# Six key projections of a hybrid decoder block: computed ahead by seven products and read back

## The chip, the core and the metric

The kernel runs on one core of a Trainium2 chip. The metric is the time of one execution on the device in microseconds (us); the lower the better. Five engines work side by side, each through its own instructions in order: TensorE (PE; its weight loads are shown as PEld), VectorE (DVE), ScalarE (ACT), GpSimd (POOL) and SyncE (SP), whose queue issues most DMAs here. They hand work over with semaphores.

## The reference, cut to what matters

A decoder block over 1024 tokens of 1024 channels: a normalised input h, a wide projection of h into many parts, two token mixers (retention over chunks, and dilated window attention in three groups of four heads), gates, and an MLP. The change concerns the keys of the attention, `ak`, 128 columns of the projection for each head:

```python
proj = h @ w_in                       # (1024, 1024) @ (1024, columns)
aq, ak, av = parts[4 + 3 * gi], parts[5 + 3 * gi], parts[6 + 3 * gi]      # per group gi
s = einsum(qs, kb) * (dh ** -0.5) + bias          # scores in a window, per head
p = exp(s - max(s)) / sum;  o = einsum(p, vb)     # groups merged by log-sum weights afterwards
```

## The kernel before, in words

Every float32 matrix product is made of three products of rounded halves (`mm3`, L215): each operand is split into a high half (a rounding copy on ScalarE) and a low half (a subtraction on VectorE), and TensorE adds low x high, high x low and high x high in PSUM. `split_w` (L206) does this for a weight tile of 128 x 1024.

Two ways of projecting stand in the kernel. The **direct** one (`proj_mm`, L503; `proj_gen`, L508) projects h on 128 columns: 8 k-steps of 6 matmuls, 48 matmuls of 512 columns. The other one, in the **queries' stage** (`queries_keys`, L1186, with the class `Blocks`, L238), takes two such column blocks at once as a 2 x 2 block product with seven products instead of eight: 7 x 4 x 3 = 84 matmuls for what costs 2 x 48 = 96 directly. Its operands from h are sums made once (`XA`); those from the weights are summed and split on VectorE and ScalarE while TensorE works (`prep`, L249), and results are combined on the way out of PSUM (`post`, `a_out`, L1136) and written to DRAM. `PAIRS` (L1110) lists what it computes: retention queries and keys ("r"), half of the retention gates ("s"), the attention's queries ("a"), and branch gates ("g"); 22 pairs.

The stages run in this order: attention values of group 0 and of groups 1 and 2, queries' stage, retention values, retention over 4 heads x 8 chunks (`chunk`, L748), attention, attention output, retention output, output projection, MLP.

The **attention** runs twice, for a pair of heads each (`pair` 0 and 1). In a pair there are six combinations of group g and head a (`combos`, L1767): (1,0) (1,1) (2,0) (2,1) (0,0) (0,1). `att_step(pair, i)` (L1769) projects the keys of combination i directly and, woven between the k-steps (`weave`, L524), computes the scores of combination i-1 (`scores_gen`, L1481): three PSUM banks of scores for group 1, two for group 2, four for group 0, each bank followed by the addition of the bias on VectorE (L1508, L1512). Behind that stand `k_split` (L1473), which splits the new keys out of PSUM, and `scores_end` (L1515): maxima on VectorE (L1518 to L1526), their negation `ng` (L1528), and eight exponentials on ScalarE (L1531). `cover_step` (L1809) does the same beside a gate's direct projection; its steps 0 and 1 cover the last scores, the weights of the groups (`weights`, L1601) and the scaling of P (`pscale`, L1632), and from step 2 on the products with the values (PV; `pv_stream`, L1701) are woven with gate projections. Pair 0's PV ends in the first step of pair 1.

What a step needs from DRAM stands in its list of loads. `Steps.run` (L71) keeps three raw tiles of 512 KB in flight on SP: a new load is issued when an earlier tile has been split (`prepare`, L93). For a step that isn't `manual`, `prepare` splits the loads of the next step, and the weights of the one after, ahead of the body. For a `manual` step the body gets a function, `args[0]`, and what it is given is split where the body calls it: `args[0](3)` splits the loads of the next step at that place. Instructions are issued in the order in which the program writes them, on every engine. Before, all steps of `att_step` but the first of each pair, and `cover_step` 0, are not manual.

The bias tables (`bias_load`, L1442) are six small DMAs issued at the end of each pair's first step. The `result_sums` (L612) prepare operands of the retention output: for the last half of the channels eight DMAs from DRAM to DRAM on POOL, four copies and four accumulations, which were issued in a row in the first attention step (L1789).

Of the kernel before, what the change touches and what calls it, by code (L numbers as in the profile page):

```python
# [21 lines left out]
H = 4  # L22
# [111 lines left out]
def block_kernel(ctx, tc, io, stop=None, dbg=None):  # L134
# [716 lines left out]
    aq_d = {(p, g, a): dram.tile([P, S], F32, name=f"aqd{p}{g}{a}") for p in range(2) for g in range(3) for a in range(2)}  # L851
    h12_d = [dram.tile([P, 2, 512], F32, name=f"h12d{m}") for m in range(4)]
# [257 lines left out]
    PAIRS = [{"r": r_pairs, "a": a_pairs, "g": g_pairs, "s": s_pairs}[i].pop(0) for i in "rsrarsrarsrarsraggagga"]  # L1110
# [3 lines left out]
    def a_load(q, part):  # L1114
        pair = PAIRS[q]
        src = io[{"g": "w_gate2", "a": "w_aq", "s": "w_rg2"}.get(pair[0]) or f"w_r{pair[1]}"]
# [19 lines left out]
    def a_out(q, n, x, y=None):  # L1136
# [6 lines left out]
        if pair[0] == "a" and pair[1] == 1:  # L1143
            o = OA[q][i].rearrange("p (r n i) -> p r n i", r=4, n=2)[:, :, t, :]
            view = lambda z: z.rearrange("p (i r) -> p r i", r=4)
        elif pair[0] == "a" and pair[1] == 2:
            o = OA[q][i].rearrange("p (r i) -> p r i", r=8)[:, :, 64 * t:64 * t + 64]
            view = lambda z: z.rearrange("p (i r) -> p r i", r=8)
# [223 lines left out]
    r_loads = {(0, 0): [io["w_rg"][0]], (H - 1, 7): [io["w_ak"][4]]}  # L1372
# [91 lines left out]
    def q_prep(pair, g, a):  # L1464

        def prep(raw):
            hi, lo = ring(f"qh{pair}{g}{a}"), ring(f"ql{pair}{g}{a}")
            nc.scalar.mul(hi, raw, QSCALE)
            nc.vector.scalar_tensor_tensor(lo, raw, QSCALE, fv(hi), op0=ALU.mult, op1=ALU.subtract)
            A["q", g, a] = (hi, lo)  # L1470
        return prep
# [297 lines left out]
    def att_step(pair, i):  # L1769

        g, a = combos[i]

        def body(*args):
            ps = ps_mm(f"ak{pair}{i}")
            gen = proj_gen(ps, hd.pop("w") if i == pair == 0 else args[-1])
            if i == len(combos) - 2:
                v_fetch(pair, 0)
            if i > 0:
                last = combos[i - 1]
                weave(gen, NK, scores_gen(pair, *last), len(SB[last[0]]), lag=2)  # L1780
            elif pair == 0:
# [13 lines left out]
            if i == 0:  # L1795
                A["st"] = A["p"].tile([P, 3, 8, 4], F32, tag="st", name=f"st{pair}")
                bias_load(pair)
            later_loads()
            if i == 0 and pair == 1:
                banks_sc()  # L1800
            else:
                k_split(pair, g, a, ps)
            if i > 0:
                scores_end(pair, *last)
                if last[1] == 1:
                    stats_out(pair, last[0])
        return body

    def cover_step(pair, n):  # L1809


        i = COVER[pair][n]

        def body(*args):
            if n == 2:
                banks_pv((("mm", "ac2", "ac3", "s", "ac0", "ac1"), ("ac0", "ac1", "s", "ac2", "ac3", "mm"))[pair])
                v_fetch(pair, 2)
            ps = ps_mm(f"gate0{i}")
            gen = proj_gen(ps, args[-1])
            if n == 0:  # L1820
                v_fetch(pair, 1)
                weave(gen, 6, scores_gen(pair, *combos[-1]), len(SB[0]), lag=2, rest=False)
                drain(gen)
                later_loads()
                for j in range(2):
                    vs_high(pair, 0, j)
                t = ring(f"g0{i}s", F32)
                nc.scalar.copy(t, flat(ps))
                A["gate", 0] = t, t
                scores_end(pair, *combos[-1])  # L1830
                weights(pair)
                pscale(0, 0)
            elif n == 1:
                drain(gen)
# [9 lines left out]

    for pair in range(2):
        for i, (g, a) in enumerate(combos):
            steps.add(att_step(pair, i),
                      ([] if i == pair == 0 else [wsplit(io["w_ak"][g * 4 + 2 * pair + a])]) +
                      ([(aq_d[pair, *combos[i - 1]], q_prep(pair, *combos[i - 1]))] if i > 0 else []),
                      manual=i == 0)  # L1850
        for n in range(len(COVER[pair])):
            more = [(aq_d[pair, *combos[-1]], q_prep(pair, *combos[-1]))] if n == 0 else []
            steps.add(cover_step(pair, n), more + [wsplit(io["w_gate"][len(COVER[0]) * pair + n])], manual=n > 0)
# [860 lines left out]
def pack(x, c, w_ada, b_ada, norm1_g, w_in, rel_bias, ret_gn_g, ret_gn_b,  # L2714
# [3 lines left out]
    att = w[:, 6144:10752].reshape(1024, 3, 3, 512)  # L2718
    rg = w[:, 4096:6144].reshape(1024, 4, 512)
# [16 lines left out]
        "w_ak": _cols(att[:, :, 1].reshape(1024, 1536)),  # L2736
# [29 lines left out]
```

## Time and profile before

| | |
|---|---|
| median of 3 runs | 2183.61 us (2181.96 to 2184.4) |
| the profiled execution's own time | 2182.82 us |
| its span in the trace | 2181.1 us |
| granted TensorE clock, mean | 0.998 |
| queries' stage | about 149 to 568 us of the span |
| attention | about 942 to 1251 us |

A row of the timeline has the start, the time from the first start to the last end of the merged instructions, engine, line, operation, output<-inputs, shape and count, and in brackets the idle time before it and what ended it. A row of a group (by tile) has minimum/median/maximum in ns and the first and last start. A row of windows has the busy time of each engine in the stretch with the number of instructions, then the granted clock, the DMA engines' busy share and GB/s. TensorE's pipelined matmuls overlap in such rows, so the distance of starts is the price of one, not its duration.

### The profile page before, as it was taken

What the parts mean: (1) busy time and instruction counts of PE and PEld (TensorE: products, weight loads), DVE (VectorE), ACT (ScalarE), POOL (GpSimd) and SP (SyncE); (2) the same over time, 40 slices, a digit from 0 to 9 for tenths busy, and PEclk for the clock granted to TensorE, in tenths of its full rate; (3) what the DMA queues carried; (4) which work ended last, traced back from release to release, by engine and by line L of the source; (5) the groups of instructions that cost most, each with busy time, mean ns of one, the idle gap of its engine ahead of it and who ended that gap; (6) DMA issues with size and microseconds to landing.
All of it is one profiled execution on the core that took longest, in us unless ns stands there. A gap on an engine that the chain in (4) does not pass through costs nothing.

```text
span 2181.1 us, 27045 instructions
## 1 busy us (share of the span) xinstructions
PE 2147.4 (98%) x10034; PEld 1784.6 (82%) x10034; DVE 1479.0 (68%) x2281; ACT 947.1 (43%) x1715; POOL 178.4 (8%) x192
## 2 busy tenths in 40 slices
PE   7999999999999999999999999999999999999998
PEld 5888888888888888888888888888878888788887
DVE  6756777767566678854655644677876665887855
ACT  4533322333334566654644525434554455433412
POOL 0101111100000334410000000001000000000003
PEclk9999999999999999999999999999999999999999
DMA  9869998734687758977323366653054445645322
GB/s 382 231 193 297 289 328 266 217 136 155 223 297 287 257 181 242 263 222 186 105 81 108 98 250 210 224 184 130 35 202 159 154 143 188 240 138 173 109 87 78
DMA packets 161891, 422.55 MB, mean 194 GB/s; under 512 B 27734, under 2 KB 55645, under 8 KB 157662
## 3 DMA queue, kind: packets, MB, share of 16 engines
q1 hardware_dynamic: 151902, 372.57, 48.4%
q0 software_dynamic: 9856, 48.24, 10.1%
q8 instruction: 79, 1.29, 0.2%
q14 instruction: 54, 0.44, 0.1%
HBM read 325.71 MB, written 160.32 MB: 223 GB/s over the span
## 4 chain that ended last, share of the span: by engine, by line
PE 90%; DVE 4%; ACT 2%; DMA 1%; issue 1%; POOL 0%; SPq 0%; POOLq 0%; DVEq 0%; ACTq 0%
PE qap L219 6%; PE qap L223 6%; PE qap L221 6%; PE fp L219 4%; PE fp L223 4%; PE fp L221 4%; PE ak L219 2%; PE ak L221 2%; PE ak L223 2%; PE f2a L221 2%; PE f2a L223 2%; PE f2a L219 2%; PE rg L221 1%; PE rg L219 1%; PE rg L223 1%; PE va L221 1%
## 5 line engine op out<-in xcount | busy, mean ns | idle before, releaser
L219 PE MATMUL qap<-hh,qaw 128*128 128x512 f32 x264 | 102.8, 389 | 0.1
L221 PE MATMUL qap<-hl,qaw 128*128 128x512 f32 x264 | 102.7, 389 | 0.0
L223 PE MATMUL qap<-hh,qaw 128*128 128x512 f32 x264 | 102.7, 389 | 0.0
L656 POOL TENSOR_TENSOR j<-qk,j 128x512 fp32r<-128x512 f32 x32 | 48.3, 1513 | 311.7 <-ACT j L655 311.7
L2117 POOL TENSOR_TENSOR accnf<-accnf,sqnf 128x256 f32<-128x256 f32 (+1 forms) x18 | 16.6, 921 | 613.2 <-ACT sqnf L2116 613.2
L2221 ACT ACTIVATE a<-a 128x512 f32<-128x512 f32 x48 | 30.3, 632 | 78.0 <-DVE a L2220 78.0
L219 PEld LDWEIGHTS qap<-hh,qaw 128*128 128x128 f32 x264 | 49.6, 188 | 10.8 <-DVE qat L310 0.5
L221 PEld LDWEIGHTS qap<-hl,qaw 128*128 128x128 f32 x264 | 49.5, 188 | 10.3
L223 PEld LDWEIGHTS qap<-hh,qaw 128*128 128x128 f32 x264 | 49.6, 188 | 10.3
L2410 ACT CAST w2h<-w2s 128x512 fp32r<-128x512 f32 x36 | 22.4, 621 | 78.2 <-DVE w2s L2448 78.2
L2117 POOL TENSOR_TENSOR accn<-accn,sqn 128x512 f32<-128x512 f32 x12 | 15.5, 1294 | 496.0 <-ACT sqn L2116 496.0
L276 DVE TENSOR_TENSOR fw<-w1r,fw 128x512 fp32r<-128x512 f32 x48 | 32.9, 688 | 33.2 <-ACT fw L266 33.2
L1531 ACT ACTIVATE P<-P,ng 128x128 f32<-128x128 f32 (+1 forms) x96 | 41.9, 438 | 29.5 <-DVE ng L1528 29.5
L276 DVE TENSOR_TENSOR qaw<-wa,qaw 128x512 fp32r<-128x512 f32 x66 | 45.0, 686 | 11.1 <-ACT qaw L266 11.1
L1309 DVE SCALAR_TENSOR_TENSOR cossin<-cossin,cb 128x1024 f32<-128x1024 f32 x32 | 39.0, 1220 | 16.4 <-DMA cossin<-in_w_ada_dram 16.4
L219 PE MATMUL fp<-h2h,fw 128*128 128x512 f32 x128 | 50.0, 390 | 0.0
L1955 DVE TENSOR_TENSOR rwl<-rwl,rwh 128x1024 fp32r<-128x1024 f32 x25 | 30.2, 1221 | 29.0 <-ACT rwh L1985 29.0
L221 PE MATMUL fp<-h2l,fw 128*128 128x512 f32 x128 | 49.8, 389 | 0.0
L223 PE MATMUL fp<-h2h,fw 128*128 128x512 f32 x128 | 49.8, 389 | 0.0
L219 PE MATMUL roa<-rh,rwl 128*128 128x512 f32 x128 | 49.8, 389 | 0.0
L221 PE MATMUL roa<-rl,rwh 128*128 128x512 f32 x128 | 49.8, 389 | 0.0
L223 PE MATMUL roa<-rh,rwh 128*128 128x512 f32 x128 | 49.8, 389 | 0.0
(3093 smaller groups left out, 7138.1 us busy)
## 6 DMA issues: line engine op xcount, KB each, us to landing
cossin<-in_w_ada_dram SPq DMA_DIRECT2D x32, 512.0 KB, 5.3
v<-vd SPq DMA_DIRECT2D x32, 512.0 KB, 5.7
w1r<-in_w_ff_dram SPq DMA_DIRECT2D x32, 512.0 KB, 4.8
vd<-vo SPq DMA_DIRECT2D x24, 512.0 KB, 6.3
xsd<-as SPq DMA_DIRECT2D x24, 512.0 KB, 2.8
w2r<-in_w_ff2s_dram SPq DMA_DIRECT2D x24, 512.0 KB, 7.6
em<-in_w_ada_dram SPq DMA_DIRECT2D x16, 512.0 KB, 10.2
wrvs<-in_w_rv_dram POOLq DMA_DIRECT2D x16, 512.0 KB, 11.1
```

What stands on the lines that cost most here:

```text
L219: nc.tensor.matmul(o, wl, xh, start=first, stop=False, skip_group_check=skip)
L221: nc.tensor.matmul(o, wh, xl, start=False, stop=False, skip_group_check=skip)
L223: nc.tensor.matmul(o, wh, xh, start=False, stop=last, skip_group_check=skip)
L276: nc.vector.tensor_sub(t[:, 512:], src, fv(t[:, :512]))
L656: nc.gpsimd.tensor_sub(t[:, 1], src, fv(t[:, 0]))
L1309: nc.vector.scalar_tensor_tensor(t, t, 1.0, cb, op0=ALU.mult, op1=ALU.mult, accum_out=mods[:, j:j + 1])
L1531: nc.scalar.activation(v, v, AF.Exp, bias=ng[:, blk:blk + 1], accum_out=st[:, g, blk, 2 + a:3 + a])
L1955: nc.vector.tensor_sub(lo, fv(lo), fv(hi))
L2117: (nc.vector if f == 7 else nc.gpsimd).tensor_add(G["acc", key], G["acc", key], sq)
L2221: nc.scalar.activation(o, o, AF.Relu)
L2410: nc.scalar.copy(hi, src)
```

## The change

Of each group and pair of heads, the keys of head a = 0 move to the queries' stage: three more pairs ("k", g), each with the two column blocks of group g for pair 0 and pair 1, computed by seven products and written to DRAM (`ak_d`). `PAIRS` has 25 entries. In the attention the keys of a = 0 are read back and split (`k_prep`), those of a = 1 are still projected directly, three instead of six a pair.

The attention's steps are cut differently. `att_first` projects the keys of (1,1). Then four half steps `att_step(pair, 0..3)` follow, and two gate half steps, "s" and 0: a direct projection now stretches over two of them, four k-steps in each, and each weaves the scores of one combination; a = 0 first. All of them are manual, and call `args[0](3)` behind the weaving: an even half step splits the next queries there, an odd one the next weights, the next read-back keys and the next queries. `cover_step` 1 now calls it too, ahead of its k-steps, and in step 0 the copy of gate 0 stands behind `scores_end`. Of the eight result sums, one is issued in each of the half steps 2 and 3, "s", 0, 1, 2, 3 of pair 0 and in pair 1's first step.

```diff
+    ak_d = {(p, g): dram.tile([P, S], F32, name=f"akd{p}{g}") for p in range(2) for g in range(3)}
...
-    PAIRS = [{"r": r_pairs, "a": a_pairs, "g": g_pairs, "s": s_pairs}[i].pop(0) for i in "rsrarsrarsrarsraggagga"]
+    k_pairs = [("k", g) for g in range(3)]
+    PAIRS = [{"r": r_pairs, "a": a_pairs, "g": g_pairs, "s": s_pairs, "k": k_pairs}[i].pop(0)
+             for i in "rsrarsrarsrarsrakggakggak"]
...
+            elif pair[0] == "k":
+                dst = ak_d[i, pair[1]]
...
+    def k_prep(pair, g, a):
+
+        def prep(raw):
+            hi, lo = ring(f"kh{pair}{g}{a}"), ring(f"kl{pair}{g}{a}")
+            nc.scalar.copy(hi, raw)
+            nc.vector.tensor_sub(lo, raw, fv(hi))
+            A["k", g, a] = (hi, lo)
+        return prep
...
+    def att_first(pair):
+
+        g, a = combos[1]
 
         def body(*args):
-            ps = ps_mm(f"ak{pair}{i}")
-            gen = proj_gen(ps, hd.pop("w") if i == pair == 0 else args[-1])
-            if i == len(combos) - 2:
-                v_fetch(pair, 0)
-            if i > 0:
-                last = combos[i - 1]
-                weave(gen, NK, scores_gen(pair, *last), len(SB[last[0]]), lag=2)
-            elif pair == 0:
+            ps = ps_mm(f"ak{pair}0")
+            gen = proj_gen(ps, args[-1] if pair else hd.pop("w"))
+            if pair == 0:
                 args[0](1, True)
...
                 u_final(H - 1)
-                for add in result_sums(slice(4, 8)):
-                    add()
+                A["sums"] = result_sums(slice(4, 8))
                 open_att()
                 args[0](3)
             else:
-                weave_pv(gen, NK, 0, 10, args[0], lambda: k_split(pair, g, a, ps))
...
+                weave_pv(gen, NK, 0, 10, args[0])
+                result_sum()
+            A["st"] = A["p"].tile([P, 3, 8, 4], F32, tag="st", name=f"st{pair}")
+            bias_load(pair)
             later_loads()
-            if i == 0 and pair == 1:
+            k_split(pair, g, a, ps)
+            if pair == 1:
                 banks_sc()
...
+    def weave_scores(pair, i, lag=1, n=NK // 2):
+
+        weave(itertools.islice(A["gen"], NK // 2), n, scores_gen(pair, *combos[i]), len(SB[combos[i][0]]), lag=lag)
+
+    def scored(pair, i):
+        scores_end(pair, *combos[i])
+        if combos[i][1] == 1:
+            stats_out(pair, combos[i][0])
+
+    def att_step(pair, i):
+
+        g, a = combos[i + 3 - i % 2]
+
+        def body(*args):
+            if i % 2 == 0:
+                A["ps"] = ps_mm(f"ak{pair}{i}")
+                A["gen"] = proj_gen(A["ps"], args[-1])
+            if i == 2:
+                v_fetch(pair, 0)
+            if i > 1:
+                result_sum()
+            weave_scores(pair, i, 2 if i == 0 else 1)
+            args[0](3)
+            later_loads()
+            if i % 2:
+                drain(A["gen"])
+                k_split(pair, g, a, A["ps"])
+            scored(pair, i)
+        return body
...
+            if n == "s":
+                A["ps"] = ps_mm(f"gate0{i}")
+                A["gen"] = proj_gen(A["ps"], args[-1])
+                weave_scores(pair, len(combos) - 2)
+                args[0](3)
+                later_loads()
+                scored(pair, len(combos) - 2)
+                return
...
             if n == 0:
                 v_fetch(pair, 1)
-                weave(gen, 6, scores_gen(pair, *combos[-1]), len(SB[0]), lag=2, rest=False)
+                weave_scores(pair, len(combos) - 1, 0, 2)
+                args[0](3)
                 drain(gen)
                 later_loads()
                 for j in range(2):
                     vs_high(pair, 0, j)
+                scores_end(pair, *combos[-1])
                 t = ring(f"g0{i}s", F32)
                 nc.scalar.copy(t, flat(ps))
                 A["gate", 0] = t, t
-                scores_end(pair, *combos[-1])
                 weights(pair)
                 pscale(0, 0)
             elif n == 1:
+                args[0](3)
                 drain(gen)
...
+    def rows_load(pair, i):
+        c = combos[i]
+        k = [(ak_d[pair, c[0]], k_prep(pair, *c))] if c[1] == 0 else []
+        return k + [(aq_d[pair, *c], q_prep(pair, *c))]
...
     for pair in range(2):
...
+        steps.add(att_first(pair), k_load(combos[0][0], pair) if pair else [], manual=True)
+        for i in range(len(combos) - 2):
+            steps.add(att_step(pair, i), (k_load(combos[i + 3][0], pair) if i % 2 == 0 else []) + rows_load(pair, i), manual=True)
+        for n in ("s", *range(len(COVER[pair]))):
+            more = rows_load(pair, len(combos) - (1 if n == 0 else 2)) if n in ("s", 0) else []
+            w = [wsplit(io["w_gate"][len(COVER[0]) * pair + (0 if n == "s" else n)])] if n != 0 else []
+            steps.add(cover_step(pair, n), w + more, manual=True)
```

The host packs the keys' columns accordingly (`w_ak` for a = 1, `w_ak2` in pairs for a = 0).

More of the change, by code (lines that the diff above doesn't have):

```diff
@@ L1843, in cover_step, with k_load @@
         return body
-    for pair in range(2):
[L1846 to L1853, printed above, removed]
+    def rows_load(pair, i):
+        c = combos[i]
+        k = [(ak_d[pair, c[0]], k_prep(pair, *c))] if c[1] == 0 else []
+        return k + [(aq_d[pair, *c], q_prep(pair, *c))]
+    def k_load(g, pair):
+        return [wsplit(io["w_ak"][2 * g + pair])]
+    for pair in range(2):
+        steps.add(att_first(pair), k_load(combos[0][0], pair) if pair else [], manual=True)
[5 more added lines that the diff above has]
+            steps.add(cover_step(pair, n), w + more, manual=True)
     G = {}
```

33 lines of the change are left out of this document (14 added, 19 removed).

## The prediction

> **What bounds the kernel now.** I read the page first: engine shares, then the chain that ended last.
>
> ```profile
> PE 2147.4 (98%) x10034; PEld 1784.6 (82%) x10034; DVE 1479.0 (68%) x2281; ACT 947.1 (43%) x1715; POOL 178.4 (8%) x192
> PE 90%; DVE 4%; ACT 2%; DMA 1%; issue 1%; POOL 0%; SPq 0%; POOLq 0%; DVEq 0%; ACTq 0%
> ```
>
> TensorE is busy for 2147.4 of 2181.1 us and holds 90% of the chain. A matmul less is time won, a TensorE wait more is time lost, one for one. Then the stretches that the change touches: the queries' stage, and the score stage of pair 0 and of pair 1, each from its second key projection to the first transposition of P.
>
> ```profile
> core 0: us, PE busy (x) PEld busy (x) DVE busy (x) ACT busy (x) POOL busy (x), PEclk, DMA share, GB/s
> 147.00:568.00 421.00, 420.91 (x1858) 348.22 (x1857) 301.41 (x480) 129.44 (x221) 33.62 (x48) 1.00 0.76 242
> 953.50:1047.70 94.20, 93.64 (x481) 79.60 (x480) 52.24 (x78) 46.89 (x125) 5.47 (x8) 1.00 0.74 212
> 1106.90:1200.30 93.40, 93.40 (x482) 79.64 (x481) 50.93 (x77) 44.64 (x122) 0.00 (x0) 1.00 0.31 92
> ```
>
> TensorE has no gap in any of them beyond 0.56 us, while VectorE and ScalarE are about half idle in the score stages. That idleness is spread over long steps; whether it is still enough when the steps are halved is the question.
>
> **The matmuls.** The first row is the first product group of the queries' stage, the second the first matmul behind that stage; the next two bound one whole projection with nothing woven in (second gate of pair 0).
>
> ```profile
> L219 PE MATMUL qap<-hh,qaw x264: 389/389/499, 149.2 to 565.0; 128*128 128x512 f32 x132
> 568.43 0.39 PE L219 MATMUL va<-vwh,hl 128*128 128x512 f32 x1
> 1036.87 0.62 PE L219 MATMUL gate<-hh,raw_8495l 128*128 128x512 f32 x2
> 1047.76 0.60 PE L1653 MATMUL sf<-ct,P 128*128 128x128 f32 x4
> ```
>
> 22 pairs of 84 matmuls take 568.43 - 149.2 = 419.2 us, 19.06 a pair; three more cost 57.2 us. A direct projection (48 matmuls) takes 10.89 us; six less save 65.3. Net **-8.1 us**. The three added pairs bring sums, splits and four evictions each on VectorE, at 301/421 = 72% there and hidden today under a TensorE with 0.09 us of gaps. An average pair has 301.4/22 = 13.7 us of VectorE in 19.06 of TensorE, so I take nothing; with that cover gone, up to 41 us of VectorE would show. Their six writes and six read-backs of 512 KB replace six weight loads, so the score stages move the same bytes from HBM; nothing.
>
> **What is moved.** Before, every step split the next weights and the next queries ahead of its own weaving. Now att_step and cover_step call args[0](3) behind the weaving. VectorE and ScalarE work in the written order, so the split of the next weights (L209, L210) stands behind the bias add of the step's last score bank on VectorE, and behind the eight exponentials of the step before on ScalarE. The first matmul of the next projection (L219) reads the low half. I price this with one step of before: two score banks, the two k-steps between them, the last bank; VectorE's query split, weight split, adds, reductions; the exponentials from first to the split behind them. First group 1 (three banks), then groups 2 (two banks) and 0 (four).
>
> ```profile
> 972.17 0.28 PE L219 MATMUL sc<-kh,ql 128*128 128x256 f32 x1
> 972.88 0.63 PE L219 MATMUL ak<-hh,raw_7985l 128*128 128x512 f32 x2
> 975.63 0.28 PE L219 MATMUL sc<-kh,ql 128*128 128x256 f32 x1
> 979.09 0.22 PE L219 MATMUL sc<-kh,ql 128*128 128x128 f32 x1
> 980.38 0.69 PE L219 MATMUL ak<-hh,raw_7985l 128*128 128x512 f32 x2
> ```
>
> ```profile
> 977.11 1.23 DVE L1469 SCALAR_TENSOR_TENSOR ql<-raw,qh 128x1024 fp32r<-128x1024 f32 x1 [4.64 <-ACT qh L1468]
> 978.25 1.22 DVE L210 TENSOR_TENSOR raw_8170l<-raw,raw_8170h 128x1024 fp32r<-128x1024 f32 x1
> 979.39 1.88 DVE L1508 TENSOR_TENSOR P<-sc,bias 128x512 f32<-128x512 f32 x3
> 984.27 0.68 DVE L1523 TENSOR_REDUCE st<-P 128x4 f32<-128x512 f32 x1
> 986.11 0.17 DVE L1528 TENSOR_SCALAR ng<-st 128x8 f32<-128x8 f32 x1
> 997.97 1.21 DVE L1526 TENSOR_REDUCE st<-P 128x8 f32<-128x1024 f32 x1
> 999.22 0.17 DVE L1528 TENSOR_SCALAR ng<-st 128x8 f32<-128x8 f32 x1
> 1025.46 0.28 DVE L1518 TENSOR_REDUCE st<-P 128x1 f32<-128x128 f32 x1
> 1027.70 0.17 DVE L1528 TENSOR_SCALAR ng<-st 128x8 f32<-128x8 f32 x1
> ```
>
> ```profile
> 986.31 0.40 ACT L1531 ACTIVATE P<-P,ng 128x128 f32<-128x128 f32 x1 [3.22 <-DVE ng L1528]
> 989.84 1.04 ACT L1468 ACTIVATE qh<-raw 128x1024 fp32r<-128x1024 f32 x1
> 990.79 1.03 ACT L209 CAST raw_8278h<-raw 128x1024 fp32r<-128x1024 f32 x1
> 999.42 0.40 ACT L1531 ACTIVATE P<-P,ng 128x128 f32<-128x128 f32 x1 [2.62 <-DVE ng L1528]
> 1002.52 1.05 ACT L1468 ACTIVATE qh<-raw 128x1024 fp32r<-128x1024 f32 x1
> 1027.91 0.41 ACT L1531 ACTIVATE P<-P,ng 128x128 f32<-128x128 f32 x1 [3.62 <-DVE ng L1528]
> 1031.77 1.03 ACT L209 CAST raw_8600h<-raw 128x1024 fp32r<-128x1024 f32 x1
> ```
>
> So a bank of two wide blocks costs TensorE 0.71 us, one of four narrow blocks 1.29, two k-steps 2.75 (1.36 + 1.39 behind a bank). VectorE passes a 1024-wide split every 1.14 us, an add every 0.6; maxima with ng take 2.0, 1.4 and 2.4 us for groups 1, 2, 0. ScalarE needs 3.5, 3.1 and 3.9 us for the exponentials and 0.95 for each 1024-wide high half. A hop between engines I take as 0.05.
>
> **Half step 1 to 2** (pair 1, counted from the end of half step 0's last bank). VectorE: last add to 0.8, query low half to 1.95, maxima to 3.95. ScalarE: exponentials to 7.5, high half of the weights to 8.45. TensorE: k, k, bank, k, bank, k, last bank end at 2.75 + 0.71 + 1.39 + 0.71 + 1.39 + 1.29 = 8.23. VectorE then: last add to 9.05, weight low half to 10.25; TensorE goes on at 10.3. **Loss 2.05.**
> **Half step 2 to 3** (zero at 8.23): behind the weights come key, query and direct-key splits and the maxima, to 7.4; exponentials to 10.95, next query's high half 11.9, low half 13.1. TensorE: restart 2.05, two k-steps, 1.29, 1.39, 1.29, 1.39 end at 10.2, two k-steps at 12.9, then the bank waits for 13.15. **Loss 0.25.**
> **Half step 3 to "s"**: TensorE ends at 18.55 (the last bank is followed by a k-step here); maxima to 14.5, exponentials to 17.65, high half 18.6, low half 19.85, restart 19.9. **Loss 1.35.**
> **"s" to cover 0** (zero at 18.55): maxima to 6.1, exponentials to 9.25, query high half 10.2; four banks end at 9.7, their last adds 10.45, query low half 11.65; cover 0's first bank stands one k-step behind, at 11.05. **Loss 0.65.**
> **Cover 0 to 1**: maxima to 14.05, exponentials to 17.95, high half 18.9, low half 20.15; TensorE ends at 18.65. **Loss 1.55.**
>
> **Start of PV.** The rows are ng and the first scaling of P (5.6 us apart), and the stall that PV has already.
>
> ```profile
> 1038.66 0.17 DVE L1528 TENSOR_SCALAR ng<-st 128x8 f32<-128x8 f32 x1
> 1044.25 1.33 DVE L1637 TENSOR_SCALAR P<-P,wt 128x128 f32<-128x128 f32 x5
> 1202.45 0.66 PE L1653 MATMUL pt100(4, 1, 4)_10312<-ct,P 128*128 128x128 f32 x4 [1.04 <-DVE ptl100(0, 0, 0)_10290 L1658]
> ```
>
> Counted from cover 1's start, maxima end at 2.4, scaling starts 5.6 later plus 0.95 for gate 0's copy, now behind the exponentials, and ends at 10.1; the third gate's split follows, low half to 12.3. TensorE needs PV at 10.9, and VectorE's copy of gate 1 starts 1.3 late. Between 0 and 1.3, I take **1.2** on top of the 1.04.
>
> Pair 1 loses 2.05 + 0.25 + 1.35 + 0.65 + 1.55 + 1.2 = 7.05 us.
>
> **Pair 0 and the bias.** Its bias tables are issued behind the first key step. The first row is the add that waited for them, then their issue, then the six-DMA groups' time to landing.
>
> ```profile
> 966.73 1.89 DVE L1508 TENSOR_TENSOR P<-sc,bias 128x512 f32<-128x512 f32 x3 [2.86 <-DMA bias<-biasd]
> 957.71 3.08 SPq L1455 DMA_DIRECT2D bias<-biasd  x6
> DMA to landing us min/median/max: 4.2/5.0/8.0
> ```
>
> Before, this wait hid: query (1,1) had been split ahead of the adds. Now that split stands behind them, and half step 1's first bank reads it. One more raw load precedes the tables on SP (it waits for the query's low half), 1.1 us, and group 1's table is the third of six at 0.51: 957.71 + 1.1 + 1.0 = 959.8. Without the result sums in that stretch I take the median 5.0: adds 964.8 to 966.65, split to 967.8, bank at 967.85 instead of 965.25: **2.6**; 1.8 by 4.2 us, 5.6 by 8.0. Half step 1 to 2 then costs 2.25. Pair 0: 2.6 + 2.25 + 0.25 + 1.35 + 0.65 + 1.55 + 1.2 = 9.85. The result sums themselves, eight 1 MB transfers, go out one by one on POOL, which has nothing else here, and are read only behind the attention; I take nothing for them, their slowing other loads is the last rival but one.
>
> **Sum**: -8.1 + 7.05 + 9.85 = +8.8 us on the profiled execution's 2182.8 (span 2181.1 and 1.7 around it): **2191.5**. The median shown is 2183.6, 0.8 higher.
>
> **A stall that becomes longer than it is.** The longest wait of before inside the busy part, and the stretch behind it:
>
> ```profile
> PE fp L219 <- DVE ft2nacc L310: 3.3, 1, 3.3
> 1592.00:1596.00 4.00, 2.98 (x9) 2.39 (x10) 3.27 (x6) 2.60 (x6) 0.00 (x0) 0.77 0.70 258
> ```
>
> After 3.3 us without matmuls the granted clock was 0.77 for 4 us: about 0.9 us of work lost in that window. The 0.56 us gap of pair 0's window left it at 1.00. Mine of up to 2.6 lie between; by the nearer end nothing, by the other 0.9 or more for each such wait (three of them, 2.7). The Trainium skill, "TensorE: Matmul & The Clock Gate", section "What's actually happening", says that an idle window of about 3.4 us halves the clock; by that rule only a late bias (5.6) would pay it, and the row of 3.3 us agrees roughly.
>
> **Rivals.**
> *Only the written order costs* (not slower). If ScalarE's high halves come in time (exponentials or maxima earlier than I counted), the end of half step 1 costs an add, a split and hops, 2.0, and that of half step 3 2.0 - 1.39 = 0.6; the others vanish. 2 x 2.6 = 5.2, so 2182.8 - 8.1 + 5.2 = 2179.9. For it: both engines half idle in the windows. Against: each chain add, split, maxima, exponentials, split has no free microsecond within 8.23 us.
> *All covered* (faster): the next weights' low half is ready when TensorE asks, in every half step: 2174.7. It decides when the losses, at all the hand-overs, sum to under 8.1 us, that is under 0.65 each over thirteen. For it: no wait over 0.56 in these windows before. Against: the add and the split cannot start before the last bank ends.
> *Late data*: the bias lands as late as before (5.6), the three long waits lower the clock (2.7), and read-backs queue behind the 1 MB sums (a few us): +14 to +18, about 2198.
> *The sums' move does nothing*: within the above.
>
> **How the numbers follow.** My case 0.60 (2187 to 2196: each of thirteen waits off by some 0.3, the bias between 1.8 and 5.6); written order only 0.15; all covered 0.10; late data 0.15. A measurement can tell about 0.2%, 4.4 us. Faster by more than that: all covered and a third of the written-order case, 0.15. Within: the rest of that case and the low end of mine, 0.20. Slower: 0.65. The range leaves out all covered and the far end of late data: 2178 to 2200.
>
> **What would show it.** In the waits of TensorE: L219 on the split of L210, six times (two of about 2.1, two of 1.4, two of 1.5 us), and sc on the query's low half in half step 1 of pair 0 behind a DMA wait of the bias. The two score windows lose 32.7 us of matmuls each but shrink by only 23 to 26; the queries' stage grows by 57 without gaps. I am wrong if L210 ends before TensorE asks, if the gaps of the score stages stay under 8.1 us in total, or if the queries' stage shows gaps.

## The result and the profile after

The changed kernel takes **2207.97 us** (median of four runs, 2203.51 to 2209.95), the kernel before beside it 2184.01 (2181.96 to 2184.9). The ratio is 1.0107, with a 95% interval of 1.0094 to 1.0120: slower, as forecast, but by nearly three times as much. The profiled execution has a span of 2205.9 us against 2181.1, so 24.8 us are to be found where the prediction had 8.8.

First the page of the kernel after: engine shares, and the chain that ended last.

```profile
PE 2147.6 (97%) x9998; PEld 1781.4 (81%) x9998; DVE 1505.0 (68%) x2323; ACT 956.8 (43%) x1736; POOL 177.1 (8%) x192
PE 85%; DVE 6%; DMA 4%; ACT 3%; issue 1%; POOL 0%; SPq 0%; POOLq 0%; DVEq 0%; ACTq 0%
```

36 matmuls are gone, yet TensorE is busy as long as before, which says that some ran slowly, and its share of the chain fell from 90% to 85%: DMA has 4% where it had 1%, VectorE 6% where it had 4%. Then the three stretches by windows: the queries' stage, and the two score stages, from the first matmul of the second key projection to the transpositions of P into the first PV bank. The columns are those of the prediction's table.

```profile
147.00:625.00 478.00, 477.72 (x2108) 395.22 (x2107) 335.32 (x528) 144.75 (x248) 33.71 (x48) 1.00 0.71 226
1010.80:1095.40 84.60, 66.90 (x337) 55.85 (x336) 47.75 (x75) 43.66 (x122) 5.49 (x8) 0.92 0.82 229
1155.40:1224.70 69.30, 62.74 (x341) 52.53 (x340) 46.19 (x73) 41.33 (x119) 0.00 (x0) 1.00 0.42 113
```

The queries' stage is full: it grew by 57.3 us (the first matmul behind it starts at 625.7, before at 568.4) and has 0.28 us of gaps. Pair 0's score stage shrank only from 94.25 to 84.7 us (-9.5), with 17.7 us of idle TensorE and a granted clock of 0.92; pair 1's from 93.8 to 69.3 (-24.5; counted in every run to the last of these transpositions, 0.3 us further than pair 0's), with 6.6 us idle. The two starts of PV add 0.8 and 0.75. The sum, 57.3 - 9.5 - 24.5 + 1.55, is 24.85: the whole difference. Next TensorE's waits, by line and by what ended them (total, times, longest).

```profile
PE sc L219 <- DVE ql L1474: 15.2, 7, 6.1
PE ak L219 <- DVE raw_9662l L210: 1.9, 1, 1.9
PE ak L219 <- DVE raw_8534l L210: 1.9, 1, 1.9
PE gate L219 <- DVE raw_8861l L210: 1.2, 1, 1.2
PE gate L219 <- DVE raw_10069l L210: 1.2, 1, 1.2
PE gate L219 <- DVE raw_8693l L210: 1.1, 1, 1.1
PE gate L219 <- DVE raw_9903l L210: 1.0, 1, 1.0
PE pt000(4, 1, 4)_9186 L1667 <- DVE ptl000(0, 0, 0)_9164 L1672: 1.8, 1, 1.8
```

The six waits on the weights' low half that the prediction named are there, at 1.9, 1.05 and 1.2 us. What it did not have is the first row: 15.2 us for the low half of queries. The timeline of the kernel after shows two of them in pair 0, at half step 1 and at the first bank of (0,0), and what stands before each (start, duration, the idle time before it and what ended that).

```profile
1016.11 4.64 SPq L1460 DMA_DIRECT2D bias<-biasd  x6
1025.40 1.88 DVE L1522 TENSOR_TENSOR P<-sc,bias 128x512 f32<-128x512 f32 x3 [8.64 <-DMA bias<-biasd]
1028.47 0.58 PE L219 MATMUL sc<-kh,ql 128*128 128x256 f32 x1 [5.58 <-DVE ql L1474]
...
1047.98 2.29 SPq L1568 DMA_DIRECT2D vl<-vad  x2
1050.38 1.75 SPq L84 DMA_DIRECT2D raw<-aqd  x1
1063.73 1.06 ACT L1473 ACTIVATE qh<-raw 128x1024 fp32r<-128x1024 f32 x1 [7.12 <-DMA raw<-aqd]
1066.10 0.58 PE L219 MATMUL sc<-kh,ql 128*128 128x256 f32 x1 [6.09 <-DVE ql L1474]
```

Both are waits for DMAs, one engine removed: the waits table names VectorE, but VectorE waited 8.64 us for the bias, and ScalarE 7.12 for the queries of (0,0). And this is POOL's queue, first of the kernel after, then of the kernel before: the eight result sums.

```profile
1015.54 0.58 POOL L604 DMA_DIRECT2D yt<-y  x1 [16.41 <-DMA y<-on]
1024.71 0.82 POOL L605 DMA_DIRECT2D yt<-y  x1 [8.59 <-DMA yt<-y]
1025.26 0.82 POOL L604 DMA_DIRECT2D yt<-y  x1
1036.91 0.82 POOL L605 DMA_DIRECT2D yt<-y  x1 [10.84 <-DMA yt<-y]
...
1062.54 0.53 POOL L604 DMA_DIRECT2D yt<-yt  x1 [12.00 <-DMA yt<-y]
1069.37 0.84 POOL L605 DMA_DIRECT2D yt<-y  x1 [6.30 <-DMA yt<-yt]
```

```profile
958.17 0.58 POOL L604 DMA_DIRECT2D yt<-y  x1 [16.29 <-DMA y<-on]
966.89 0.82 POOL L605 DMA_DIRECT2D yt<-y  x1 [8.14 <-DMA yt<-y]
...
1011.74 0.84 POOL L605 DMA_DIRECT2D yt<-y  x1 [6.07 <-DMA yt<-yt]
```

The first sum starts at 1015.54, which is 958.17 plus the 57.3 us of the longer queries' stage. Nothing was spread: a sum waits for the data of the sums before it or for nothing (the third row), and never for anything of the step in which it is written. The last view of the kernel after is the clock around the two waits.

```profile
1024.00:1028.00 4.00, 0.00 (x0) 0.00 (x0) 2.60 (x4) 0.00 (x0) 1.37 (x2) 0.82 0.59 95
1028.00:1032.00 4.00, 3.52 (x11) 3.10 (x12) 2.92 (x5) 1.61 (x7) 0.00 (x0) 0.50 1.01 215
1032.00:1036.00 4.00, 4.00 (x24) 3.59 (x23) 0.69 (x1) 3.89 (x12) 0.00 (x0) 0.83 0.92 381
1064.00:1068.00 4.00, 1.90 (x9) 1.90 (x10) 3.18 (x3) 1.69 (x2) 0.00 (x0) 0.51 0.99 366
1068.00:1072.00 4.00, 4.00 (x18) 3.48 (x18) 1.72 (x4) 3.45 (x17) 0.84 (x1) 0.63 0.63 148
```

The busy microseconds times the clock that was missing: 3.52 x 0.50 + 4.00 x 0.17 + 1.90 x 0.49 + 4.00 x 0.37 = 4.85 us. Pair 0's stage lost 23.1 us against its matmuls (84.7 - 94.25 + 32.7): 17.7 idle, 4.85 by the clock, the rest in first matmuls behind a wait.

**Theory 1**: the result sums, which still run through pair 0's score stage, make the bias and the queries of (0,0) late, and the new order lets TensorE feel it. **Theory 2**, the rival: the order on SP and the depth of its loads make them late, and the sums have no part in it. For the hand-overs, **theory A**: the waits on the weights come from ScalarE, which does their high half behind eight exponentials, against the possibility that only the place on VectorE matters.

### The profile page after: what moved, and what is told of

Read it like the earlier page. It is cut to its first block, busy times and chain, and to the rows that moved or that the text cites. A ratio compares the mean times of both kernels' runs of the same rounds, so it can differ in the third digit from the quotient of the medians.

```text
span 2205.9 us, 27077 instructions
## 1 busy us (share of the span) xinstructions
PE 2147.6 (97%) x9998; PEld 1781.4 (81%) x9998; DVE 1505.0 (68%) x2323; ACT 956.8 (43%) x1736; POOL 177.1 (8%) x192
## 4 chain that ended last, share of the span: by engine, by line
PE 85%; DVE 6%; DMA 4%; ACT 3%; issue 1%; POOL 0%; SPq 0%; POOLq 0%; DVEq 0%; ACTq 0%
PE qap L223 7%; PE qap L219 7%; PE qap L221 7%; PE fp L219 4%; PE fp L221 4%; PE fp L223 4%; PE f2a L221 2%; PE f2a L219 2%; PE f2a L223 2%; DMA raw<-aqd 2%; PE rg L221 1%; PE rg L219 1%; PE rg L223 1%; PE va L221 1%; PE va L219 1%; PE va L223 1%
## 5 line engine op out<-in xcount | busy, mean ns | idle before, releaser
L219 PE MATMUL qap<-hh,qaw 128*128 128x512 f32 x300 | 116.8, 389 | 0.3 <-DVE qat L310 0.3
L221 PE MATMUL qap<-hl,qaw 128*128 128x512 f32 x300 | 116.7, 389 | 0.0
L223 PE MATMUL qap<-hh,qaw 128*128 128x512 f32 x300 | 116.7, 389 | 0.0
L219 PEld LDWEIGHTS qap<-hh,qaw 128*128 128x128 f32 x300 | 56.3, 188 | 12.3 <-DVE qat L310 0.7
L221 PEld LDWEIGHTS qap<-hl,qaw 128*128 128x128 f32 x300 | 56.3, 188 | 11.8
L223 PEld LDWEIGHTS qap<-hh,qaw 128*128 128x128 f32 x300 | 56.3, 188 | 11.7
L276 DVE TENSOR_TENSOR qaw<-wa,qaw 128x512 fp32r<-128x512 f32 x75 | 51.2, 687 | 21.1 <-ACT qaw L266 21.1
L266 ACT CAST qaw<-wa 128x512 fp32r<-128x512 f32 x75 | 45.2, 616 | 33.2 <-PE qap L223 20.4
```

The source lines that it names most:

```text
L219: nc.tensor.matmul(o, wl, xh, start=first, stop=False, skip_group_check=skip)
L221: nc.tensor.matmul(o, wh, xl, start=False, stop=False, skip_group_check=skip)
L223: nc.tensor.matmul(o, wh, xh, start=False, stop=last, skip_group_check=skip)
L266: nc.scalar.copy(t[:, :512], src)
L276: nc.vector.tensor_sub(t[:, 512:], src, fv(t[:, :512]))
```

## The experiments

Every edit is one to the changed kernel. Medians are of four runs (the last of five), each against the kernel before on the same chip (2182.9 to 2183.5). "Stage 0" and "stage 1" are the two score stages, 84.7 and 69.3 us in the changed kernel.

**The sums in a row again** (e1).

```diff
-                A["sums"] = result_sums(slice(4, 8))
+                A["sums"] = []
+                for add in result_sums(slice(4, 8)):
+                    add()
```

> The changed kernel with its eight result sums written in a row again, at the place where the first of them stands. Theory 1 (POOL has nothing to wait for between the sums, so they run one behind the other as fast as they land, written in a row or one per half step): same times of issue on POOL as in the changed kernel within 2 us, the two waits of about 6 us stay, 2204 to 2211 us. If spreading them did slow or relieve the loads: more than 3 us away from 2208, and the eight issues close together.

2205.02 us (2203.02 to 2207.34; ratio 1.0099, 1.0084 to 1.0114). POOL's queue in this run:

```profile
1015.57 0.58 POOL L604 DMA_DIRECT2D yt<-y  x1 [16.43 <-DMA y<-on]
1024.41 0.82 POOL L605 DMA_DIRECT2D yt<-y  x1 [8.26 <-DMA yt<-y]
...
1069.58 0.84 POOL L605 DMA_DIRECT2D yt<-y  x1 [6.31 <-DMA yt<-yt]
```

The same times within 1.2 us all through: one sum per half step is the same program on POOL as eight in a row. The two long waits were 4.98 and 3.45 us here and stage 0 took 80.3 us, so the second wait varies between executions by some 3 us; the ranges of the two kernels' times overlap.

**The sums held back** (e2, e6, e10). A small addition on POOL reads what the attention has just made, and the eight sums stand behind it: behind the weights of pair 0 (e2), or behind its second gate (e6).

```diff
-                A["sums"] = result_sums(slice(4, 8))
+                A["sums"] = []
...
                 weights(pair)
+                if pair == 0:
+                    tie = cst.tile([P, 8], F32, name="tie")
+                    nc.gpsimd.tensor_add(tie, A["w", 0][:, :, 0], A["w", 0][:, :, 1])
+                    for add in result_sums(slice(4, 8)):
+                        add()
```

> The eight result sums held back until the weights of pair 0 are made (an addition on POOL that reads them stands ahead of the sums). Theory 1 (the sums share the DMA engines with the bias tables and with the queries of group 0, so that both land late): the bias is there about 3 us earlier and the queries of (0,0) land in about 8.4 us in place of 13.2, the wait of 5.6 us shrinks to about 2.5 and that of 6.1 to about 1, the clock stays at 1.00 in pair 0's score stage, 2193 to 2199 us. Theory 2 (the order on SP and the depth of the loads make them late, the sums have no part in it): both waits stay, 2205 to 2211.

Stage 0 fell to 70.7 us, and TensorE's waits for queries, in the run with held sums, to a third:

```profile
PE sc L219 <- DVE ql L1474: 5.0, 5, 2.2
```

The wait behind the bias is 2.20 us, the one for (0,0) is gone, and the clock stays at 1.00 in stage 0. That is theory 1, and theory 2, by which the sums have no part in it, falls. Yet the whole took 2211.29 us (1.0127, 1.0111 to 1.0142). The gain went in the later stages; one row of the same group of matmuls, of the second feed-forward product, first in the kernel after, then with held sums:

```profile
L219 PE MATMUL f2a<-b00h,w2l x8: 389/389/389, 1874.2 to 1883.1; 128*128 128x512 f32 x8
```

```profile
L219 PE MATMUL f2a<-b00h,w2l x8: 395/396/397, 1868.5 to 1877.6; 128*128 128x512 f32 x8
```

The retention output starts 13.4 us earlier (1303.5 against 1316.9), this group only 5.7, and each matmul takes 396 ns in place of 389. So the second question was where the slower matmuls come from.

> The eight result sums held back as in the run before (e2_sums_held), but behind the copy of the second gate of pair 0, some 4 us later. In that run pair 0's score stage fell from 84.7 to 70.7 us, and yet the whole did not get faster, because from about 1240 us to the end each 128x512 matmul took 392 to 396 ns in place of 389. Theory P (the slower matmuls belong to sums that run beside PV): 392 to 396 ns again, 2208 to 2213 us. Theory Q (they belong to that one program or its execution): 389 ns to the end, pair 0's stage 70 to 72 us, 2192 to 2197.

2211.76 us (1.0130, 1.0115 to 1.0145), 396 ns again, stage 0 at 74.3. By this run alone theory P would stand; but both kernels share the new tile, so two more were made: the sums held with the addition written to an existing place (e10), and the changed kernel with the tile and the addition, its sums written where they were (e11).

```diff
-                    tie = cst.tile([P, 8], F32, name="tie")
-                    nc.gpsimd.tensor_add(tie, A["w", 0][:, :, 0], A["w", 0][:, :, 1])
+                    tie = A["p"].tile([P, 8, 2], F32, tag="mx", name="tie")
+                    nc.gpsimd.tensor_add(tie[:, :, 0], A["w", 0][:, :, 0], A["w", 0][:, :, 1])
```

> The eight result sums held back until the weights of pair 0 are made, as in e2_sums_held, but the small addition on POOL that holds them writes to a place that the attention's pool already had, not to a new tile of 32 bytes a partition among the constants. Theory R (the 392 to 396 ns a matmul in the three runs with held sums come from the new tile, which moves what is laid out behind it, not from the sums): 389 ns to the end, pair 0's stage 70 to 72 us, 2192 to 2196 us. Theory P (sums beside PV make them): 392 to 396 again, 2209 to 2213.

> The changed kernel with its sums where they are, and with the small addition on POOL and its new tile of 32 bytes a partition alone. Theory R: 392 to 396 ns a matmul from about 1240 us on, 14 to 16 us on top of the changed kernel, 2219 to 2224 us. Theory P: 389 ns, 2205 to 2210.

Held without a new tile: **2197.04 us** (2196.06 to 2197.37; 1.0062, 1.0047 to 1.0077), 389 ns. The tile and the addition in the changed kernel: 2214.32 (2213.01 to 2218.0; 1.0145, 1.0130 to 1.0160), 396 ns, with stage 0 at 75.4. The row of each, in that order:

```profile
L219 PE MATMUL f2a<-b00h,w2l x8: 389/389/390, 1863.7 to 1872.6; 128*128 128x512 f32 x8
```

```profile
L219 PE MATMUL f2a<-b00h,w2l x8: 395/396/397, 1871.5 to 1880.7; 128*128 128x512 f32 x8
```

Theory R holds: e2 and e10 differ in nothing but the place that the addition writes, so the 32 bytes a partition made the matmuls slower, the sums did not. e11 is not the tile alone, though. POOL works in the written order, and there the addition stands between the fourth and the fifth sum:

```profile
1084.22 0.28 POOL L1881 TENSOR_TENSOR tie<-wt 128x8 f32<-128x8 f32 x1 [46.36 <-DVE wt L1637]
1084.68 0.67 POOL L604 DMA_DIRECT2D yt<-yt  x1 [0.18 <-issue]
```

It waits for the weights of pair 0, so the last four sums are held as well; the fifth was issued at 1037.47 in the changed kernel. The wait behind the bias is 5.0 us in e11, the one at (0,0) is gone, and the time stays under the 2219 to 2224 that were expected. So e10 alone shows what the sums cost without the tile: 11 us against the changed kernel and 8 against e1, net of whatever the held sums cost beside PV. Its score stages, with the columns as above:

```profile
1011.70:1083.70 72.00, 63.91 (x337) 53.31 (x337) 47.98 (x75) 43.55 (x122) 0.90 (x2) 0.98 0.50 153
1144.00:1213.10 69.10, 62.79 (x342) 52.59 (x342) 46.13 (x73) 41.32 (x119) 0.00 (x0) 1.00 0.50 132
```

With the sums out, the DMA share of stage 0 is 0.50 (0.82 in the changed kernel), its idle time 8.1 us (17.7), and the two stages are now much alike.

**The value loads behind the queries** (e4).

```diff
-            if i == 2:
-                v_fetch(pair, 0)
...
                 args[0](3)
+                v_fetch(pair, 0)
                 later_loads()
                 scored(pair, len(combos) - 2)
```

> The two value loads of group 0 (512 KB each) are issued behind the loads of half step s in place of ahead of half step 2. Theory 2 (these loads, right ahead of the queries of (0,0) on SP, make them late): TensorE's wait of 6.1 us goes, and the clock stays up behind it, 2199 to 2203 us. Theory 1 (the result sums do it): the wait shrinks by 1 to 3 us, 2204 to 2207. If the values then come late themselves, the high halves in the step of the first gate wait, and the start of PV is later than in the changed kernel.

2200.62 us (2197.66 to 2206.47; 1.0081, 1.0063 to 1.0100), stage 0 at 75.2. The wait at (0,0) is gone in the profiled run, the one behind the bias (4.7 us) is not. This is what theory 2 expected of the run, so the value loads have a share in the second wait, more than theory 1 gave them; but with the sums held (e10) the same loads stand right ahead of the queries and that wait does not come. Sums and value loads together make it: the queries of (0,0) landed in 13.2 us beside both (11.3 in e1), in 7.6 without the sums (e10), in 6.1 ahead of the value loads (e4).

**The query of (1,1) ahead of half step 0** (e7).

```diff
+            if i == pair == 0:
+                args[0](3)
             weave_scores(pair, i, 2 if i == 0 else 1)
             args[0](3)
```

> Only the query split of (1,1) stands ahead of half step 0's weaving in pair 0, where every such split stood before; the rest as in the changed kernel. Theory 1 (the late bias costs only because that split stands behind the bias adds): TensorE's wait of 5.6 us at the first bank of half step 1 is under 1, the clock stays at 1.00 there, pair 0's stage falls from 84.7 to 77 to 79, 2200 to 2203 us. Rival (a late bias stalls TensorE anyway, by the score banks that stay full until the adds are done): a wait of 3 to 5 us stays on the adds, 2205 or more.

2201.05 us (2200.89 to 2203.29; 1.0084, 1.0067 to 1.0101), stage 0 at 78.3. The waits of this kernel:

```profile
PE ak L219 <- DVE raw_8534l L210: 5.4, 1, 5.4
PE sc L219 <- DVE P L1522: 0.8, 1, 0.8
```

The 5.58 us at half step 1 became 0.8, as theory 1 has it, and 3.5 of them came back one hand-over later: the exponentials are late by the same bias, and the weights' high half stands behind them (1.9 became 5.4), with the clock at 0.50 behind that wait. The time is what theory 1 expected, but in part by luck: the second wait was 3.3 us in this run, and e1, where it was 3.45, had a stage 0 of 80.3, only 2.0 us more.

**The weights split ahead of the exponentials** (e3, and e14 with held sums).

```diff
             args[0](3)
+            if i % 2 == 0:
+                args[0](1, True, 1)
             later_loads()
```

The third argument is new: it takes the loads of one step further (the same in half step s).

> In every even half step the weights of the projection after next are split right behind the query split, so ahead of that half step's exponentials. Theory A (the waits on the weights' low half come from ScalarE, which does the high half only behind eight exponentials): the six waits of TensorE on L210 (1.9, 1.05 and 1.2 us in pair 0, 1.9, 1.0 and 1.2 in pair 1, 8.3 in all) vanish, and the time falls by 6 to 8 us, to 2200 to 2202; the two data waits of pair 0 stay. Theory B (only the place behind the last bias add on VectorE matters): the early split stands behind an add as well, so the wait moves to the next bank's query, and the time falls by under 3 us.

> Held sums as in e10_held_mx, and the weights of the projection after next split ahead of the exponentials as in e3_weights_far. With the data on time this shows what the six waits on the weights' low half cost by themselves. Theory A (they are lost time that goes when the high half no longer stands behind eight exponentials): 6 to 8 us under e10_held_mx, 2189 to 2191. Theory C (ScalarE and VectorE pass the work of a half step to each other in one chain, so a wait taken off the weights comes up at the next query): no wait on L210 is left, but both score stages fall by only 2 to 2.5 us each, 2192 to 2194.

2199.75 us (1.0078, 1.0061 to 1.0094) for e3, with stages of 77.6 and 67.1; 2193.16 (2190.3 to 2195.19; 1.0044, 1.0029 to 1.0059) for e14, with 69.5 and 68.1. In neither is there a wait on L210 in the score stages. This is e14's row of queries, 5.8 us in e10:

```profile
PE sc L219 <- DVE ql L1474: 11.0, 10, 2.4
```

Of 7.8 us of waits on the weights 5.2 come up again at the next query. The 8.2 us by which e3 is under the changed kernel are as much as theory A expected, but 7.1 of them are in pair 0's stage, where the second data wait was 3.9 us in that run; pair 1's, with its data on time, fell by 2.2. e14 is 3.9 us under e10, with stages shorter by 2.5 and 1.0. Theory A names the releaser rightly and the price wrongly; theory C holds, though its 2 to 2.5 us a stage were too much for pair 1.

**All splits ahead of the weaving, in pair 1** (e12) **and, with held sums, in both** (e13): the order of the kernel before.

```diff
+            if pair == 1:
+                args[0](3)
             weave_scores(pair, i, 2 if i == 0 else 1)
             args[0](3)
...
```

The same stands ahead of the weaving of half step s and of cover 0; in e13 without the condition.

> In pair 1 alone every half step's splits stand ahead of its weaving again, as they stood in the kernel before. Theory 1 (the hand-over losses come from the place of the splits): the waits of pair 1's stage go but for what the start of PV costs, the stage falls from 69.3 to 63 to 65 us, and the whole to 2202 to 2204. Rival (the chain from the last bank over maxima, exponentials and weights to the first scaled P sets the end of the stage): the stage falls too, but the wait at the start of PV grows from 1.8 to 3.5 us or more, with the clock lowered behind it, and the whole stays at 2205 to 2208.

> Held sums as in e10_held_mx, and the splits ahead of the weaving in both pairs. If Theory R and Theory 1 hold: pair 0's stage 62 to 66 us, pair 1's 63 to 65, 2181 to 2186 us, level with the kernel before. If the start of PV takes it back in both pairs: 2190 to 2194. If Theory P holds: 2198 to 2208.

2215.54 us (1.0152, 1.0135 to 1.0169), stage 1 at 73.5 in place of 69.3, and 2210.98 (1.0126, 1.0110 to 1.0141), stages of 76.4 and 73.6. The stages grew, which no expectation had, so the old order costs more; the wait at the start of PV grew as well, from 1.8 to 3.7 us, as the rival had it. VectorE in e12 shows why:

```profile
1177.15 0.17 DVE L1542 TENSOR_SCALAR ng<-st 128x8 f32<-128x8 f32 x1
1181.96 1.23 DVE L1474 SCALAR_TENSOR_TENSOR ql<-raw,qh 128x1024 fp32r<-128x1024 f32 x1 [4.64 <-ACT qh L1473]
1183.10 1.28 DVE L1522 TENSOR_TENSOR P<-sc,bias 128x512 f32<-128x512 f32 x2
1185.67 0.17 DVE L1542 TENSOR_SCALAR ng<-st 128x8 f32<-128x8 f32 x1
1190.04 1.23 DVE L210 TENSOR_TENSOR raw_9848l<-raw,raw_9848h 128x1024 fp32r<-128x1024 f32 x1 [4.20 <-ACT raw_9848h L209]
...
1197.23 0.17 DVE L1542 TENSOR_SCALAR ng<-st 128x8 f32<-128x8 f32 x1
```

The split that stands ahead waits for its high half, which stands behind the exponentials of the step before; the bias adds stand behind the split; the next exponentials need those adds. VectorE and ScalarE work in turns, VectorE idle for 4 to 5 us in each, and one turn takes 8.5 us (1177.15 to 1185.67) and 11.6 (to 1197.23), against 8.2 of matmuls in half step 1. In the kernel before a step had 13.7 us (the starts of two projections, 968.1 and 981.8), and the turn fitted.

**Edits together**: e8 is e3, e4 and e7 with the bias issued ahead of the raw loads; e9 holds the sums as well (with the new tile); e15 is e14 with e7.

> Four edits together: weights of the projection after next split ahead of the exponentials, value loads of group 0 behind the queries, query (1,1) split ahead of half step 0, bias tables issued ahead of the raw loads. If they add (8 for the weights and 7 for the values, as measured, 5 to 6 for the query, 1 for the bias): 2185 to 2189 us, level with the kernel before, pair 0's stage near 66. If the result sums only make the next load late instead: one wait of 3 to 6 us stays in pair 0's stage, and 2190 to 2195.

> The four edits with the result sums held back as well. If held sums bring slower matmuls behind pair 0 (Theory P): 2192 to 2200 us, with 392 to 396 ns in the later stages. If not (Theory Q): pair 0's stage 62 to 65 us, 2179 to 2184, level with or faster than the kernel before.

> The same with the query split of (1,1) ahead of half step 0's weaving in pair 0. The wait of 3.0 us at the first bank of half step 1 (the bias without the sums) goes. If it is lost time: 2 to 3 us under e14_held_far, and nothing of it comes back at the start of PV (1.8 us). If the chain to the first scaled P sets the end of the stage: the wait at the start of PV grows to 3 us or more and the time is within 1 us of e14_held_far.

e8 took 2203.33 us (1.0092, 1.0077 to 1.0107), above both expectations and no less than e3, e4 and e7 took alone. Stage 0 is 78.8 us. Waits of 4.4 and 2.6 us for queries stay in half steps 2 and s, and this is the stage's end:

```profile
PE sf L1667 <- DVE P L1651: 4.4, 1, 4.4
PE pt000(4, 1, 4)_9186 L1667 <- DVE ptl000(0, 0, 0)_9164 L1672: 3.1, 1, 3.1
```

Of what the hand-overs gave, the start of PV took a part: it waits for the first scaled P. e9 took 2208.68 (1.0116, 1.0101 to 1.0131), above its expectations too, with the slower matmuls, stage 0 at 65.9 and the stretch behind it, to the first key projection of pair 1, 46.0 us where it was 41.4. e15 took **2190.95** (2190.26 to 2194.26; 1.0040, 1.0026 to 1.0054), within the range of e14: the wait of 2.4 us at half step 1 is gone, but one of 3.2 us stands in half step 2 where e14 had 1.6; stage 0 went from 69.5 to 68.9, the stretch behind it from 41.3 to 42.0. It is the best form of the change that was run, and it is still slower than the kernel before.

## Why the prediction was right in direction and wrong in size

*Matmuls.* Right: 57.3 us against 57.2, the queries' stage without gaps.

*Hand-overs.* Right in place and nearly in size: 1.9, 1.05 and 1.2 us on L210 where the prediction had 2.05 (2.25 in pair 0), 1.35 and 1.55. Pair 1's stage lost 8.2 us against 5.85: a wait of 0.7 for the first key's low half and 1.6 us in longer first matmuls were not in the sum, and the waits for queries were none in half step 3, 0.9 in half step s and 0.7 in cover 0 where it had 0.25, nothing and 0.65. Their cause was told too simply. "ScalarE's high halves" behind the exponentials release the waits, but moving them (e14) gives back 3.9 of 7.8 us, and the old place is worse (e12): half a step of 8.2 us is too short for a turn of VectorE and ScalarE of 8.5 to 11.6.

*Start of PV.* 0.8 and 0.75 where 1.2 was taken.

*The step that failed* is the premise in "Pair 0 and the bias": "Without the result sums in that stretch I take the median 5.0", and with it "go out one by one on POOL ... I take nothing for them". The sums never left the stretch, since POOL has nothing else to wait for: e1 shows the same issue times for both ways of writing. The prediction had the fact in hand ("POOL, which has nothing else here") and did not ask what would hold a sum back. With the sums really out (e2, e10, e6) the bias term is 2.20, 2.96 and 3.03 us, forecast 2.6, and stage 0 is 70.7, 72.0 and 74.3 where the prediction's terms up to there give 94.25 - 32.7 + 8.65 = 70.2. Pair 0's bias tables then landed in a median of 5.0 us (e10; 3.4 in e2), as taken; with the sums in, in 7.0 (5.9 to 8.0). With them in, the bias term is 5.58, there is a second wait of 6.09 in half step s where the sum has no term (its 0.65 is for the next query, in cover 0, which cost 0.50), and 4.85 us go by the clock: together 3.0 + 6.1 + 4.85 = 13.9 of the 14.5 us by which stage 0 missed.

*The read-backs*, costed at nothing because the bytes from HBM stay the same, were not nothing: in the kernel before the queries of (0,0) were split 23 us after their issue (979.50 to 1002.52), in the changed one ScalarE is ready for them after 6.2 us (1050.38 to 1056.6), and they landed after 13.2. What counts is the time from issue to use, not the bytes.

*The clock.* The prediction priced waits of up to 2.6 us at nothing. In the profiled run of the changed kernel that held: behind its two waits of 1.9 us the clock stayed at 1.00, while behind 5.58 and 6.09 us it was 0.50 and 0.51. In other runs it did not. The first row is the window behind a wait of 1.92 us in e2 (the end of half step 1 in pair 1), the second the one around the end of a wait of 2.96 us in e10:

```profile
1160.00:1164.00 4.00, 4.00 (x11) 3.13 (x12) 4.00 (x5) 0.81 (x1) 0.00 (x0) 0.57 0.68 218
1026.00:1030.00 4.00, 3.18 (x20) 2.89 (x21) 3.34 (x6) 1.27 (x6) 0.00 (x0) 1.00 0.42 131
```

In e1 it fell to 0.50 behind both waits of 1.9 us (2 to 4 us after their end), at the same places as in the changed kernel. So the price of nothing was luck of one execution. Counted as above, by busy time in windows of 4 us, the lowered clock took 0, 1.6 and 2.9 us of stage 0 in e2, e10 and e6; without it the three stages are 70.7, 70.4 and 71.4 us, close to the forecast 70.2. The Trainium skill, "TensorE: Matmul & The Clock Gate", section "What's actually happening", puts the limit at an idle window of about 3.4 us. The waits of 5.58 and 6.09 us agree with that, the 1.92 us of e2 does not. What decides behind waits of about 2 to 3 us, these runs leave open.

*Rivals.* "Late data" was the case that came, with the mechanism named (a late bias, a lowered clock, read-backs behind the sums) and a price of 14 to 18 that was too small, since it had one long wait and "a few us" of read-backs where there were two long waits. Its chance of 0.15 was too low: the speaking row was the wait for the bias that the kernel before had already, 2.86 us behind sums that the change did not move. "All covered" and "Only the written order costs" are excluded by the waits on L210.

## What to carry to other kernels

A transfer is moved in time only by something that its own queue waits for; writing it later in the program does nothing on a queue that is otherwise empty (e1), and any instruction that waits on that queue moves all that stands behind it (e11). When a step is cut in half, take the turn that its helper engines make from one result to the next (here adds, maxima, exponentials, split) and compare it with the new step, not their busy share with the span. And where a wait is removed inside a stage, look at what ends the stage: in e8 and e9 the start of PV took part of the gain back.

## What was not expected of the hardware

A tile of 32 bytes a partition that one small addition writes made the 128x512 matmuls of the later stages take 392 to 396 ns in place of 389, in four kernels (e2, e6, e9, e11), some 14 us in all (e2 against e10: 2211.29 and 2197.04), while the windows' granted clock stayed at 1.00. The matmuls ahead of the attention kept 389 ns. That the tile moves what is laid out behind it is the likely reason, but no run varied the place by itself, so this stays open.

Eight sums of 1 MB each, from DRAM to DRAM with one or two under way, delayed a load of 512 KB issued beside them and the value loads: it landed in 13.2 us (11.3 in e1) against 7.6 in e10. The Trainium skill, "DMA: Bandwidth & Descriptors", section "Issuing engines are not separate DMA queues", says that transfers of all issuing engines run on the same 16 engines and interleave; the windows agree, with a DMA share of 0.82 in pair 0's stage and of 0.50 without the sums.
